# New tokens' share of the samples' values in one product per group, and the conv norm's channel tiles added before the partition sum

## The chip, the cores and the metric

The program runs on one core of a Trainium2 chip. The metric is the device time of one execution in microseconds (us), as the median of several runs. The core has five engines with a queue each: PE multiplies matrices (its weight loads are shown apart, as PEld), DVE and ACT do vector and activation work, POOL does vector work on SBUF only, and SP here issues every DMA. Each engine takes its instructions strictly in the order in which they were written.

## The reference, cut to what matters

One decoder layer is computed for 512 prompt tokens and for 8 samples of 4 new tokens each (32 sample tokens). The sample tokens attend to 2048 cached rows of keys and values and to their own new ones:

```python
h = rms_norm(x, norm_pre); z = h @ w_in          # q | k | v | gate | conv a | conv b | conv gate
# samples: k_all = [cached k, new k], v_all = [cached v, new v]; three dilated patterns,
# their softmaxes merged, so every output is one weighted sum over cached and new values
c = depthwise_causal_conv(u_pad, conv_dw_w, conv_dw_b)      # 512 channels
mu = mean(c); var = mean((c - mu)**2)                       # LayerNorm over the channels
c = silu((c - mu) * rsqrt(var + EPS) * g + b)
mix = concat(att * silu(g_att), (c @ conv_pw_w + conv_pw_b) * silu(g_conv))
y = x + rms_norm(mix @ w_out, norm_post)
```

The output also holds the caches, moved on by four tokens.

## The kernel before, in words

**The main line.** 544 token columns (512 + 32) are projected in 60 column tiles of `w_in` (`project`, L849), each in four steps of 24 matmuls; weights and activations are split into a high and a low part, which makes three matmuls of one. After each step comes a tick (`tick`, L767). In a tick the side generators write a piece of their work into the engines' queues: heads of the prompt's attention (rank 0), the samples' attention (rank 1), the conv branch (rank 2). So PE's queue holds steps of `z` with small pieces between them, and what a piece waits for holds up all that follows. The pieces' dates (`UTK`, `UTV`, the numbers that a generator yields) count ticks, not time.

**The weights.** For each quarter of a weight tile (`split`, L798) ACT casts the high part `wh` (L809) and POOL makes the low part `wl` (L810). Each has four buffers, and ACT and POOL run ahead of PE as far as these allow. In their queues a quarter's two instructions stand where `project` writes them: the third quarter ahead of a tile's first step, the fourth ahead of its second, the next tile's first two ahead of its third and fourth.

**The samples' values** (`v_phase`, L700). There are three groups of four heads. For each group and each of the 8 samples (24 units) PE multiplies the probabilities by the cached values: `kvf` (j = 0 to 2, written in one tick) and `kvm` (j = 3 to 6) and at last the new values `vtm` (j = 7), two ticks later. Each j is four matmuls side by side on 32 columns of the array each; j = 7 has 32 rows only, all samples' new tokens at once, with probabilities that are zero off the sample's own. Four samples fill one PSUM bank `o` (tag `acc`, one buffer). `gather` (L707) then copies the bank to `osb` on ACT (L709), PE turns it (`ot`, L713) and DVE writes the parts to `mixg` (L719).

**The conv norm** (`conv_ln`, L456). `cc` holds four tiles of 128 channels. For each half of the tokens (272 columns), PE sums over the channels by four float32 matmuls with a constant matrix into one bank (`pm`, L469); DVE subtracts the mean (L471); ACT squares (`csq`, L479); four more matmuls sum the squares (`pvar`, L483); ACT copies them (L485). Up to it, DVE makes the depthwise conv tap by tap (L442, L444).

**Bulk copies.** The cached rows are copied DRAM to DRAM in 176 pieces (`bulk`, L321). A tick issues them until the bytes sent reach START + PACE times a count of PE's columns (`mm` adds to it, L105; a float32 matmul counts four times, one with a tile position once).

**The output stage** (L1128 on) multiplies by `w_out`: `oz` for the prompt's tokens, `os` for the samples' (straight from the loaded weights `raw`, L1140).

Of the kernel before, what the change touches and what calls it, by code (L numbers as in the profile page):

```python
# [10 lines left out]
F32 = mybir.dt.float32  # L11
F32R = mybir.dt.float32r
AF = mybir.ActivationFunctionType
ALU = mybir.AluOpType
# [4 lines left out]
P = 128  # L19
# [3 lines left out]
NB = 8  # L23
NT = 4
NS = NB * NT
TOK = SEQ + NS
HT = TOK // 2
NH = 12
G4 = 4
PAST = 2048  # L30
ROW = 2 * NH * P
CW = 31
# [10 lines left out]

UTK, UTV = 3.8, 3.7

START, PACE = 4_000_000, 166.3

NF = 3

# [36 lines left out]
def body(tc, xT, xtok, gpost, w_in, w_out, ckv, cconv, relb, vecs, pww, c_oht, c_ohr, c_lmr, c_tm, c_pick,  # L86
         o_y, o_kvp, o_cp, o_cs, o_kvs):
    nc = tc.nc
# [7 lines left out]
    def dma(out, in_):  # L96
        sent[0] += 4 * math.prod(out.shape)
        return tc.keep_in_program_order(nc.sync.dma_start(out, in_))
# [4 lines left out]
    def mm(out, lhsT, rhs, start, stop, tile_position=None):  # L103
        n = math.prod(rhs.shape[1:])
        pe[0] += n * (1 if rhs.dtype == F32R or tile_position else 4)  # L105
        if tile_position is None:
            nc.tensor.matmul(out, lhsT, rhs, start=start, stop=stop)  # L107
        else:
            nc.tensor.matmul(out, lhsT, rhs, start=start, stop=stop, tile_position=tile_position)  # L109

    def tr(out, in_, eye):
        pe[0] += in_.shape[0] * 2
        nc.tensor.transpose(out, in_, eye)  # L113

    def dma_late(out, in_, delay=5):
        late.append((now[0] + delay, out, in_))
# [51 lines left out]
    def bank(tag, name):  # L168
        return (psz if tag == "z" else psa).tile([P, 512], F32, tag=tag, name=name)
# [15 lines left out]
    def V(o, i=0):  # L185
        return vec[:, o + i:o + i + 1]

    xh, xl = [], []
    ones = keep.tile([P, P], F32, name="ones")
# [46 lines left out]
    apool = ap_.enter_context(tc.tile_pool(name="att", bufs=1))  # L236
# [44 lines left out]
    lt = ip.tile([P, 3, 8, NT], F32, name="lt")  # L281
# [174 lines left out]
    def conv_ln():  # L456
        cc = mixg[3]
        def load_pw(n):
            pw = apool.tile([P, 4, P], F32, tag="pw", name=f"pw{n}")
            dma(pw, pww[:, :, n * P:(n + 1) * P])  # L460
            return pw

        pw = load_pw(1)

        for hf in range(2):
            sl = slice(hf * HT, hf * HT + HT)
            pm = bank("z", f"pm{hf}")
            for ct in range(4):
                mm(pm[:, :HT], ones, cc[:, ct, sl], start=(ct == 0), stop=(ct == 3))  # L469
            for ct in range(4):  # L470
                nc.vector.scalar_tensor_tensor(cc[:, ct, sl], pm[:, :HT], -4.0, cc[:, ct, sl], op0=ALU.mult,  # L471
                                               op1=ALU.add)
            yield
        ri = apool.tile([P, TOK], F32, tag="q", name="cri")
        for hf in range(2):
            sl = slice(hf * HT, hf * HT + HT)
            csq = [apool.tile([P, 2, HT], F32, tag="up", name=f"csq{hf}_{i}", bufs=2) for i in range(2)]
            for ct in range(4):
                nc.scalar.activation(csq[ct // 2][:, ct % 2, :], cc[:, ct, sl], AF.Square)  # L479
            yield  # L480
            pv = bank("z", f"pvar{hf}")
            for ct in range(4):
                mm(pv[:, :HT], ones, csq[ct // 2][:, ct % 2, :], start=(ct == 0), stop=(ct == 3))  # L483
            vs = apool.tile([P, HT], F32, tag="ccv", name=f"vs{hf}")
            nc.scalar.copy(vs, pv[:, :HT])  # L485
            yield
            yield from rsqrt(ri[:, sl], vs, HT, 4.0, apool, tag="up")
            yield
        for ct in range(4):
            nc.vector.tensor_tensor(cc[:, ct, :], cc[:, ct, :], ri, op=ALU.mult)  # L490
            nc.scalar.activation(cc[:, ct, :], cc[:, ct, :], AF.Identity, bias=V(V_LNB, ct), scale=V(V_LNG, ct))
            th = apool.tile([P, TOK], F32, tag="up", name=f"cth{ct}", bufs=2)
            nc.scalar.activation(th, cc[:, ct, :], AF.Tanh, scale=0.5)
            nc.vector.scalar_tensor_tensor(cc[:, ct, :], th, 1.0, cc[:, ct, :], op0=ALU.add, op1=ALU.mult)
            yield

        res = [cc[:, 0, :]] + [apool.tile([P, TOK], F32, tag="up", name=f"pwo{i}", bufs=2) for i in range(2)]
        res.append(apool.tile([P, TOK], F32, tag="q", name="pwo2"))
        for n in (1, 2, 3, 0):
            for hf in range(2):  # L500
                sl = slice(hf * HT, hf * HT + HT)
                ps = bank("z", "pwp")
                for ct in range(4):
                    mm(ps[:, :HT], pw[:, ct, :], cc[:, ct, sl], start=(ct == 0), stop=(ct == 3))
                dst = res[n]
                nc.scalar.activation(dst[:, sl], ps[:, :HT], AF.Identity, bias=V(V_PWB, n), scale=0.5)
                yield
            if n:
                yield
                pw = load_pw((n + 1) % 4)  # L510
                yield
                yield
                yield
        for n in range(1, 4):
            nc.scalar.copy(cc[:, n, :], res[n])
        state["conv"] = True
        yield
# [4 lines left out]
    smp = {}  # L522
# [35 lines left out]
    def tm_take(g, nm, tag):  # L558
        t_ = state["sp"].tile([NS, 512], F32, tag=tag, name=f"{nm}tm{g}", bufs=2 if tag == "qb" else 1)
        nc.scalar.copy(t_, smp[g][nm + "ps"][0:NS, :])  # L560
        off = ((0 if nm == "k" else NH) + g * G4) * P
        dma_late(o_kvs[:, PAST - NT:PAST, off:off + 512], t_)
        smp[g][nm + "tm"] = t_
# [136 lines left out]
    def v_phase(g):  # L700
        sp = state["sp"]
        u0 = g * 16 + 8
        pt = smp[g]["pt"]
        while state.get("v", -1) < 4 * g + 3:
            yield

        def gather(half, o):  # L707
            osb = sp.tile([P, 512], F32, tag="ktn", name=f"osb{g}_{half}")
            nc.scalar.copy(osb, o)  # L709
            yield  # L710
            ps = bank("q", f"ot{g}_{half}")
            for s in range(4):
                tr(ps[:, s * P:s * P + P], osb[:, s * P:s * P + P], ident)  # L713
            yield
            for s in range(4):
                b = half * 4 + s
                src = ps[:, s * P:s * P + P].rearrange("p (h r) -> p h r", h=G4)[:, :, NT * b:NT * b + NT]
                dst = mixg[g][:, :, SEQ + NT * b:SEQ + NT * b + NT]
                nc.vector.tensor_copy(dst, src)  # L719
            yield  # L720

        got = iter(())
        for half in range(2):
            o = bank("acc", f"o{g}_{half}")
            for s in range(4):
                b = half * 4 + s
                u = u0 + b
                load_far(u)
                load_mid(u)
                load_far(u + 1)  # L730
                far, mid = fars[u], mids[u]
                if b < 2:
                    tm_mm(g, "vk"[b])
                for j in range(8):
                    for hh in range(G4):
                        hs = slice(hh * NS, hh * NS + NS)
                        hc = slice(hh * P, hh * P + P)
                        if j < 7:
                            src = far[:, j, hc] if j < 3 else mid[:, j - 3, hc]
                            lt = pt[:, j, hs]  # L740
                        else:
                            src = smp[g]["vtm"][:, hc]
                            lt = pt[0:NS, 7, hs]
                        mm(o[hs, s * P:s * P + P], lt, src, start=(j == 0), stop=(j == 7),
                                         tile_position=(0, hh * NS))
                    if j == 2:
                        yield UTV / 2
                        if b < 2:
                            tm_take(g, "vk"[b], ("vnew", "qb")[b])
                        next(got, None)  # L750
                        load_mid(u + 1)
                if s < 3:
                    yield UTV / 2
                    next(got, None)
            yield UTV / 2 - 1 if half == 0 else 1
            got = gather(half, o)
            next(got)
            yield
        load_far(u0 + 9)
        load_mid(u0 + 9)  # L760
        smp[g]["got"] = got
# [207 lines left out]
    for n in range(N_IN):  # L969
        c = order[n]  # L970
# [6 lines left out]
        if c < 3 * NH:  # L977
            nm = "qkv"[kind]
            g, hh = divmod(h, G4)
# [89 lines left out]
    op = ctx.enter_context(tc.tile_pool(name="outp", bufs=1))  # L1069
# [76 lines left out]
    for c in range(4):  # L1146
        last = c == 3

        for bs in (((0, 1), (2,), (3,)) if last else ((0, 1), (2, 3))):
            tags = ("z", "z") if 0 in bs else ("att", "s") if 2 in bs else ("t",)  # L1150
            z = [bank(t, f"oz{c}_{b}") for b, t in zip(bs, tags)]
            for i in range(KT):
                j = c * KT + i
# [146 lines left out]
```

## Time and profile before

| | |
|---|---|
| median of 3 runs | 1174.95 us (1173.05 to 1175.88) |
| the profiled execution | 1170.97 us, its span 1169.2 us |
| PE busy | 1137.5 us (97%) |
| DVE, POOL, ACT busy | 674.0, 406.8, 378.1 us |
| DMA | 401.92 MB, mean 344 GB/s |
| granted TensorE clock, mean | 0.990 |

Busy time is the union of an engine's instructions. A float32 matmul leaves two records in the trace. In a timeline each row is a run of like instructions: start, length, engine, line, operation, output<-inputs, shape, count, and in brackets how long the engine had been idle and who ended that.

### The profile page before, as it was taken

The page shows a single profiled execution, that of the slowest core. Times are in us where ns is not written, and L with a number is a line of the kernel's source. Part 1 is how long each engine was busy: PE and PEld are TensorE (multiplying, and loading weights), DVE is VectorE, ACT ScalarE, POOL GpSimd, SP SyncE. Part 2 cuts the span into 40 slices and gives each one's busy share as a digit, 9 for nine tenths or more (in the row PEclk, how much of TensorE's full clock was granted, in tenths as well). Part 3 has the DMA queues.
Part 4 walks back from the last instruction along what each step waited for, and adds up shares of the span by engine and source line. Part 5 has one row for each costly group of instructions (what it writes and reads, how often), then busy time and mean ns, then how long its engine had stood idle before and what let it go on. Part 6 is the DMA issues. An engine that isn't in the chain of part 4 may idle for free.

```text
span 1169.2 us, 23598 instructions
## 1 busy us (share of the span) xinstructions
PE 1137.5 (97%) x9322; PEld 1029.4 (88%) x9322; DVE 674.0 (58%) x1997; ACT 378.1 (32%) x749; POOL 406.8 (35%) x353
## 2 busy tenths in 40 slices
PE   7899999999999999999999999999999999999996
PEld 7699999999999999999999999899999976776775
DVE  5209899599699988778233576994222243112136
ACT  5433333422123332331334333423222253223241
POOL 5043323344344333333322222334333445313130
PEclk9989999999999999999999999999999998999999
DMA  9899999999998998999998899889999968999966
GB/s 363 278 339 373 402 351 343 383 312 338 408 329 320 402 381 323 351 362 355 408 375 331 293 384 395 330 317 373 387 386 338 337 218 292 337 357 389 332 232 225
DMA packets 96083, 401.92 MB, mean 344 GB/s; under 512 B 15000, under 2 KB 17816, under 8 KB 89765
## 3 DMA queue, kind: packets, MB, share of 16 engines
q1 hardware_dynamic: 95972, 400.42, 93.6%
q8 instruction: 73, 1.20, 0.4%
q14 instruction: 38, 0.30, 0.1%
HBM read 388.65 MB, written 212.66 MB: 514 GB/s over the span
## 4 chain that ended last, share of the span: by engine, by line
PE 56%; DVE 2%; DMA 1%; issue 1%; POOL 0%; ACT 0%; SPq 0%; DVEq 0%; ACTq 0%; POOLq 0%
PE z L107 32%; PE oz L107 14%; PE o L109 3%; PE pwp L107 1%; PE os L109 1%; PE att L107 1%; DMA raw<-in_w_out_dram 1%; PE s L107 1%; PE t L113 1%; DVE qsc L628 1%; POOL owl L844 0%; PE kt L113 0%; PE pvar L107 0%; PE pm L107 0%; PE sn L109 0%
## 5 line engine op out<-in xcount | busy, mean ns | idle before, releaser
L107 PE MATMUL z<-xh,wh 128*128 128x272 f32 x1920 | 572.3, 298 | 8.7 <-ACT wh L894 7.6
L107 PE MATMUL z<-xh,wl 128*128 128x272 f32 x1920 | 555.0, 289 | 1.1 <-POOL wl L895 0.6
L107 PE MATMUL z<-xl,wh 128*128 128x272 f32 x1920 | 553.4, 288 | 0.0
L810 POOL TENSOR_TENSOR wl<-raw,wh 128x512 fp32r<-128x512 f32 x228 | 311.1, 1374 | 471.3 <-ACT wh L809 447.7
L107 PEld LDWEIGHTS z<-xh,wh 128*128 128x128 f32 x1920 | 363.6, 189 | 25.2 <-issue 11.0
L107 PEld LDWEIGHTS z<-xl,wh 128*128 128x128 f32 x1920 | 363.2, 189 | 1.6 <-issue 1.0
L107 PEld LDWEIGHTS z<-xh,wl 128*128 128x128 f32 x1920 | 363.0, 189 | 1.8 <-POOL wl L895 0.9
L809 ACT CAST wh<-raw 128x512 fp32r<-128x512 f32 x228 | 139.1, 617 | 181.4 <-PE z L107 106.4
L334 DVE TENSOR_TENSOR t<-z,R 128x272 f32<-128x272 f32 x96 | 42.0, 439 | 181.5 <-PE z L107 170.2
L628 DVE SCALAR_TENSOR_TENSOR qsc<-kvf,qb 128x128 f32<-128x128 f32 x288 | 125.6, 436 | 8.8
L628 DVE SCALAR_TENSOR_TENSOR qsc<-kvm,qb 128x128 f32<-128x128 f32 x288 | 112.4, 390 | 8.8
L442 DVE SCALAR_TENSOR_TENSOR mix<-up,vec,mix 128x512 f32<-128x512 f32 x120 | 107.6, 896 | 0.0
L107 PE MATMUL oz<-owl,mh 128*128 128x512 f32 x256 | 101.7, 397 | 3.7 <-POOL owl L844 3.7
L107 PE MATMUL oz<-owh,mh 128*128 128x512 f32 x256 | 103.4, 404 | 1.5 <-ACT owh L843 1.5
L107 PE MATMUL oz<-owh,ml 128*128 128x512 f32 x256 | 101.3, 396 | 0.0
L844 POOL TENSOR_TENSOR owl<-raw,owh 128x512 fp32r<-128x512 f32 x43 | 61.4, 1447 | 111.2 <-ACT owh L843 81.8
L107 PEld LDWEIGHTS oz<-owh,mh 128*128 128x128 f32 x256 | 48.5, 189 | 26.4 <-issue 8.4
L844 DVE TENSOR_TENSOR owl<-raw,owh 128x512 fp32r<-128x512 f32 x21 | 21.7, 1032 | 73.0 <-ACT owh L843 72.8
L107 PEld LDWEIGHTS oz<-owl,mh 128*128 128x128 f32 x256 | 48.7, 190 | 15.6 <-POOL owl L844 4.1
L843 ACT CAST owh<-raw 128x512 fp32r<-128x512 f32 x64 | 36.8, 618 | 78.3 <-DMA raw<-in_w_out_dram 69.4
L107 PEld LDWEIGHTS oz<-owh,ml 128*128 128x128 f32 x256 | 48.4, 189 | 10.6
L444 DVE SCALAR_TENSOR_TENSOR mix<-us,vec,mix 128x32 f32<-128x32 f32 x120 | 57.0, 475 | 0.0
(180 smaller groups left out, 991.7 us busy)
## 6 DMA issues: line engine op xcount, KB each, us to landing
out_dram<-in_ckv_dram SPq DMA_DIRECT2D x168, 1152.0 KB, 12.2
raw<-in_w_in_dram SPq DMA_DIRECT2D x119, 512.0 KB, 9.7
kvm<-in_ckv_dram SPq DMA_DIRECT2D x48, 1024.0 KB, 10.5
kvf<-in_ckv_dram SPq DMA_DIRECT2D x144, 256.0 KB, 8.2
raw<-in_w_out_dram SPq DMA_DIRECT2D x32, 512.0 KB, 9.1
out_dram<-t SPq DMA_DIRECT2D x24, 256.0 KB, 9.2
mix<-in_xtok_dram SPq DMA_DIRECT2D x4, 1024.0 KB, 14.0
xt<-in_xtok_dram SPq DMA_DIRECT2D x8, 512.0 KB, 4.7
```

Of the source, the lines that this page charges most:

```text
L107: nc.tensor.matmul(out, lhsT, rhs, start=start, stop=stop)
L109: nc.tensor.matmul(out, lhsT, rhs, start=start, stop=stop, tile_position=tile_position)
L113: nc.tensor.transpose(out, in_, eye)
L334: nc.vector.tensor_tensor(dst[:, sl], z[hf][:, :HT], R[:, sl], op=ALU.mult)
L442: nc.vector.scalar_tensor_tensor(cc[:, ct, :SEQ], up[:, j:j + SEQ], wj, cc[:, ct, :SEQ], op0=ALU.mult, op1=ALU.add)
L444: nc.vector.scalar_tensor_tensor(cs, us[:, :, j:j + NT], wj, cs, op0=ALU.mult, op1=ALU.add)
L628: nc.vector.scalar_tensor_tensor(scr, src[:, hh * P:hh * P + P], SCALE, qb[:, hh * P:hh * P + P], op0=ALU.mult, op1=ALU.mult, accum_out=sd ...
L809: nc.scalar.copy(wh, raw)
L810: nc.gpsimd.tensor_tensor(wl, raw, wh.bitcast(F32), op=ALU.subtract)
L843: nc.scalar.copy(wh, raw)
L844: (nc.vector if j % 3 == 2 else nc.gpsimd).tensor_tensor(wl, raw, wh.bitcast(F32), op=ALU.subtract)
```

## The change

Three things change. In `v_phase` the part j = 7 is taken out of all 24 units; it is computed once for each group, for all samples, in unit b = 3 ahead of j = 0 (`new_mm`, into a bank of tag `q`), copied by ACT to a new tile `ov`, and added in `gather`: where ACT copied the bank `o`, DVE now adds `ov` to each of its four parts. In `conv_ln` POOL adds the four channel tiles (three adds, `total`, in two buffers of tag `us`), and PE sums over the partitions with one matmul in place of four. PACE goes from 166.3 to 167.9.

```diff
@@ -43,7 +43,7 @@
 
 UTK, UTV = 3.8, 3.7
 
-START, PACE = 4_000_000, 166.3
+START, PACE = 4_000_000, 167.9
 
 NF = 3
 
@@ -460,13 +460,21 @@
             dma(pw, pww[:, :, n * P:(n + 1) * P])
             return pw
 
+        def total(parts, name):
+
+            a = apool.tile([P, NB * (NT + CW - 1)], F32, tag="us", name=f"ca{name}", bufs=2)[:, :HT]
+            b = apool.tile([P, NB * (NT + CW - 1)], F32, tag="us", name=f"cb{name}", bufs=2)[:, :HT]
+            nc.gpsimd.tensor_tensor(a, parts[0], parts[1], op=ALU.add)
+            nc.gpsimd.tensor_tensor(b, parts[2], parts[3], op=ALU.add)
+            nc.gpsimd.tensor_tensor(a, a, b, op=ALU.add)
+            return a
+
         pw = load_pw(1)
 
         for hf in range(2):
             sl = slice(hf * HT, hf * HT + HT)
             pm = bank("z", f"pm{hf}")
-            for ct in range(4):
-                mm(pm[:, :HT], ones, cc[:, ct, sl], start=(ct == 0), stop=(ct == 3))
+            mm(pm[:, :HT], ones, total([cc[:, ct, sl] for ct in range(4)], f"m{hf}"), start=True, stop=True)
             for ct in range(4):
                 nc.vector.scalar_tensor_tensor(cc[:, ct, sl], pm[:, :HT], -4.0, cc[:, ct, sl], op0=ALU.mult,
                                                op1=ALU.add)
@@ -479,8 +487,8 @@
                 nc.scalar.activation(csq[ct // 2][:, ct % 2, :], cc[:, ct, sl], AF.Square)
             yield
             pv = bank("z", f"pvar{hf}")
-            for ct in range(4):
-                mm(pv[:, :HT], ones, csq[ct // 2][:, ct % 2, :], start=(ct == 0), stop=(ct == 3))
+            mm(pv[:, :HT], ones, total([csq[ct // 2][:, ct % 2, :] for ct in range(4)], f"v{hf}"), start=True,
+               stop=True)
             vs = apool.tile([P, HT], F32, tag="ccv", name=f"vs{hf}")
             nc.scalar.copy(vs, pv[:, :HT])
             yield
@@ -706,7 +714,8 @@
 
         def gather(half, o):
             osb = sp.tile([P, 512], F32, tag="ktn", name=f"osb{g}_{half}")
-            nc.scalar.copy(osb, o)
+            nc.vector.tensor_tensor(osb.rearrange("p (s c) -> p s c", s=4), o.rearrange("p (s c) -> p s c", s=4),
+                                    ov[:, None, :].to_broadcast([P, 4, P]), op=ALU.add)
             yield
             ps = bank("q", f"ot{g}_{half}")
             for s in range(4):
@@ -720,6 +729,17 @@
             yield
 
         got = iter(())
+
+        ov = sp.tile([P, P], F32, tag="ov", name=f"ov{g}")
+
+        def new_mm():
+            ps = bank("q", f"ov{g}")
+            for hh in range(G4):
+                hs = slice(hh * NS, hh * NS + NS)
+                mm(ps[hs, 0:P], pt[0:NS, 7, hs], smp[g]["vtm"][:, hh * P:hh * P + P], start=True, stop=True,
+                   tile_position=(0, hh * NS))
+            return ps
+
         for half in range(2):
             o = bank("acc", f"o{g}_{half}")
             for s in range(4):
@@ -731,22 +751,21 @@
                 far, mid = fars[u], mids[u]
                 if b < 2:
                     tm_mm(g, "vk"[b])
-                for j in range(8):
+                if b == 3:
+                    new = new_mm()
+                for j in range(7):
                     for hh in range(G4):
                         hs = slice(hh * NS, hh * NS + NS)
                         hc = slice(hh * P, hh * P + P)
-                        if j < 7:
-                            src = far[:, j, hc] if j < 3 else mid[:, j - 3, hc]
-                            lt = pt[:, j, hs]
-                        else:
-                            src = smp[g]["vtm"][:, hc]
-                            lt = pt[0:NS, 7, hs]
-                        mm(o[hs, s * P:s * P + P], lt, src, start=(j == 0), stop=(j == 7),
+                        src = far[:, j, hc] if j < 3 else mid[:, j - 3, hc]
+                        mm(o[hs, s * P:s * P + P], pt[:, j, hs], src, start=(j == 0), stop=(j == 6),
                                          tile_position=(0, hh * NS))
                     if j == 2:
                         yield UTV / 2
                         if b < 2:
                             tm_take(g, "vk"[b], ("vnew", "qb")[b])
+                        if b == 3:
+                            nc.scalar.copy(ov, new[:, 0:P])
                         next(got, None)
                         load_mid(u + 1)
                 if s < 3:
```

## Rows read from the trace of the kernel before

**Rows 1.** The page's first lines: span, and busy time of each engine.

```profile
span 1169.2 us, 23598 instructions
PE 1137.5 (97%) x9322; PEld 1029.4 (88%) x9322; DVE 674.0 (58%) x1997; ACT 378.1 (32%) x749; POOL 406.8 (35%) x353
```

**Rows 2.** Waits of PE: for whom, us in total, times, longest.

```profile
PE z L107 <- ACT wh L894: 7.6, 1, 7.6
...
PE os L109 <- DMA raw<-in_w_out_dram: 0.2, 1, 0.2
```

**Rows 3.** Timeline of PE, stretches around units of the samples' values.

```profile
239.32 0.86 PE L109 MATMUL o<-kvf,spt 128*32 128x128 f32 x24
240.11 0.39 PE L107 MATMUL z<-xh,wh 128*128 128x272 f32 x1
...
246.29 1.08 PE L109 MATMUL o<-kvm,spt 128*32 128x128 f32 x32
247.30 0.42 PE L109 MATMUL o<-vtm,spt 32*32 32x128 f32 x8
247.65 0.39 PE L107 MATMUL z<-xh,wh 128*128 128x272 f32 x1
...
295.00 0.86 PE L109 MATMUL o<-kvf,spt 128*32 128x128 f32 x24
```

**Rows 4.** Groups of PE by shape: count, busy us, mean ns, idle before.

```profile
L107 PE MATMUL pm<-mix,ones 128*128 128x272 f32 x16 | 4.1, 399 | 0.0
```

**Rows 5.** Timeline of PE, the conv norm's sums.

```profile
555.79 2.10 PE L107 MATMUL pm<-mix,ones 128*128 128x272 f32 x8
...
560.75 1.99 PE L107 MATMUL pm<-mix,ones 128*128 128x272 f32 x8
...
570.12 2.00 PE L107 MATMUL pvar<-csq,ones 128*128 128x272 f32 x8
...
590.85 2.10 PE L107 MATMUL pvar<-csq,ones 128*128 128x272 f32 x8
```

**Rows 6.** Timeline of POOL around the conv norm.

```profile
548.20 1.47 POOL L810 TENSOR_TENSOR wl<-raw,wh 128x512 fp32r<-128x512 f32 x1 [0.22 <-ACT wh L809]
554.23 1.28 POOL L810 TENSOR_TENSOR wl<-raw,wh 128x512 fp32r<-128x512 f32 x1 [4.56 <-ACT wh L809]
...
564.89 1.28 POOL L810 TENSOR_TENSOR wl<-raw,wh 128x512 fp32r<-128x512 f32 x1 [7.89 <-ACT wh L809]
...
590.67 0.21 POOL L1027 COPY sk<-t 128x32 f32<-128x32 f32 x1 [6.32 <-DVE t L334]
```

**Rows 7.** Timeline of DVE: a half's end, and the conv taps' end.

```profile
289.07 0.43 DVE L997 TENSOR_TENSOR mix<-z,R 128x272 f32<-128x272 f32 x1
...
548.45 1.27 DVE L444 SCALAR_TENSOR_TENSOR mix<-us,vec,mix 128x32 f32<-128x32 f32 x1
...
550.31 0.24 DVE L444 SCALAR_TENSOR_TENSOR mix<-us,vec,mix 128x32 f32<-128x32 f32 x1
```

**Rows 8.** Timeline of ACT, the second half's squares.

```profile
581.10 1.39 ACT L479 ACTIVATE csq<-mix 128x272 f32<-128x272 f32 x4
```

**Rows 9.** Groups of POOL, DVE and ACT by shape.

```profile
L1020 POOL COPY smix<-mix 128x128 f32<-128x128 f32 x3 | 0.8, 306 | 0.0
...
L677 DVE TENSOR_TENSOR srow<-pa,srow 128x512 f32<-128x512 f32 x3 | 2.0, 680 | 0.0
...
L376 ACT COPY pt<-t 128x128 f32<-128x128 f32 x12 | 3.2, 264 | 7.3 <-PE t L113 7.1
```

**Rows 10.** Stretch of the output stage: busy us by engine, clock, DMA share, GB/s.

```profile
1000.00:1100.00 100.00, 99.79 (x450) 73.04 (x449) 21.37 (x27) 28.85 (x58) 28.23 (x21) 1.00 0.99 359
```

**Rows 11.** Chain of waits in the output stage: start, us, what.

```profile
1059.27 11.57 DMA raw<-in_w_out_dram
...
1070.88 1.05 PE os L109 x4
```

**Rows 12.** The page's DMA issues: count, KB each, us to landing.

```profile
out_dram<-in_ckv_dram SPq DMA_DIRECT2D x168, 1152.0 KB, 12.2
```

## The prediction

> **What bounds the kernel now.** I read the page's first lines, then PE's waits, then PE's timeline at the two places that change, then POOL's, DVE's and ACT's timelines there, and last the transfers.
>
> PE is busy for 1137.5 of 1169.2 us [rows 1], so all its idle time is 31.7 us. The longest single wait is 7.6 us, at the start, for the first cast weights; in the whole execution PE itself lost 0.2 us to a transfer [rows 2]. The reader is to see that no other engine holds PE up between the ramp and the last rows: POOL and ACT are busy for a third, DVE for 58% [rows 1]. Time taken off PE's queue should therefore come off the end, as long as nothing that PE waits for comes later than now.
>
> **1. The new tokens' part leaves the units.** In the timeline of one unit the four cached parts j = 3 to 6 take 246.29 to 247.30, and j = 7 takes 247.30 to 247.65, when the next weight matmul starts: 0.35 us [rows 3]. Do the four parts get dearer when z follows them directly? Three parts that are followed by z take 239.32 to 240.11, 0.79 us or 0.264 each with the turn to z in it; four at that price are 1.05, against 1.01 now [rows 3]. So a unit saves 0.31 to 0.35 us; I take 0.35, since the 1.01 us hold a turn already (to j = 7). The code makes 24 units of three groups and eight samples: 8.4 us gone, 7.4 at the low price.
>
> Added are three times the same eight records, between a z and a j = 0 part, which has no like in the trace. From below: eight records at the mean price of the 32, a quarter of 1.01 us, 0.25; from above: the 0.35 us of j = 7, and once more the 0.1 us by which it exceeds that quarter, 0.45. I take 0.35, the row of the same records: 1.05 us. Net 6.0 to 7.7 us, I take 7.4.
>
> The Trainium skill, TensorEngine Tiling (Array Packing), Tiling Modes, says that a change of the tiling mode drains the engine, and this speaks against a block of its own shape between two others. The trace agrees in so far as the 0.35 us of j = 7 exceed that quarter [rows 3]; by the rule each block costs the 0.45, and the net is 7.1 us.
>
> The copy of `ov` is a 128x128 copy from PSUM on ACT, 0.26 us [rows 9], three times, in an engine that is busy for 32%; its reader comes two ticks later at least. In `gather` ACT's copy becomes an add on DVE, 128x512 with an input in PSUM: 0.68 us by the nearest row [rows 9], six times, 4.1 us. What hides it: DVE must have read the bank before the next unit's first matmul. At the first half's end the next part starts at 295.00, and the last values, written two ticks ahead (7.0 us from 239.32 to 246.29) and 1.36 us long, are done by about 289.4 [rows 3], and DVE is then just past its 289.07 item, ahead of a tick's taps [rows 7]; in DVE's order the add falls right behind that item, so it ends at about 290.2, 4.8 us early. Behind the add wait three pairs of taps and the second half's scaling; PE needs that bank a tile later. Cost taken: nothing; without that cover at most 6 x 0.7 = 4 us.
>
> **2. The conv norm.** Each sum is eight records. The second one shows their step: 1.99 us [rows 5], of which the last record takes 0.40 [rows 4], so seven steps in 1.59, 0.228 us each. Six go: 1.37 us; four sums [rows 5] make 5.5 us. The first sum, 2.10 us, gives steps of 0.24 and 5.8 us; all eight records spread over 1.7 us give 0.21 and 5.1.
>
> Added are twelve POOL adds of 128x272 float32. The trace has none on POOL. Bounds: below, a 128x128 copy, 0.31 us [rows 9]; above, a 128x512 subtraction, 1.28 us, or 1.47 us while DVE runs taps [rows 6]. The second is the same kind of instruction with 1.9 times the columns: 0.68 us, I take 0.7, so 2.1 us for a sum's three. PE now waits for POOL, and all of PE's queue stands behind that wait; POOL in turn must have the inputs, must be past the weight part written ahead of the tick, and for the second sum on must wait until PE has read the buffer two adds back. Place by place, before PE gets there:
>
> - First mean: POOL is free at 549.67 (548.20 + 1.47) and next busy at 554.23 with a weight part that stands behind the tick [rows 6]; the last tap ends at 550.55 [rows 7]. Adds end near 552.0, PE arrives at 555.79 [rows 5]: 3.8 us early.
> - Second mean: the part of 554.23 ends at 555.51; the buffer is free when PE has done the first sum, about 556.4; adds end at 558.5. PE arrives 1.37 earlier than now, 559.4: 0.9 early at 0.7 us, 0.8 late at 1.28 us.
> - First variance: behind the part of 564.89 [rows 6], moved up by two sums to 562.15 to 563.4; adds end at 565.5; PE arrives at 570.12 - 2.74 - 0.35 = 567.0: 1.5 early.
> - Second variance: squares end at 582.5 [rows 8], and POOL is idle from 584.35 to 590.67 [rows 6]. All of this moves up by some 4.5 us with PE, the adds end about 4 us early.
>
> So at 0.7 us nothing is late; at 1.28 us some 1 us is lost. The weight parts behind the adds slip by up to 4 us and are used by PE only two steps, 6 us, later. I take 5.5 less 0.1: 5.4 us.
>
> **3. PACE.** The count falls by 84 x 128 columns for the samples and 12 x 272 x 4 for the norm, 23,808, of some 2.3 million (an estimate: the z, oz and os records alone are 2 million): 1.0%, and PACE rises by 0.96%. So the copies end at the same place of the program, in 1% less time. This matters where transfers are close: in the output stage the DMA share is 0.99 at 359 GB/s [rows 10], and the chain of waits runs through one weight load of 11.57 us that lands just as PE needs it [rows 11]; PE lost 0.2 us there [rows 2]. A copy is 1152 KB [rows 12], 3.3 us at that rate. If one falls ahead of such a load where now it falls behind, PE waits about 3 us. Bounds: nothing, or once in each of four column groups, 12 us. Only one load has no slack in the chain, and copies come neither more nor fewer, so I take less than half of one copy: 1.3 us lost.
>
> **Sum.** 7.4 + 5.4 - 1.3 = 11.5 us. The profiled execution took 1170.97 us (1.8 around its span) and would take 1159.5. It lies 4.0 us below the median of the runs, 1174.95; I carry that over: 1163.4 us.
>
> **Rivals.**
> - *Weight loads late in the output stage.* For it: the rows of part 3. Against it: one bare load, 0.2 us of waiting. If all four column groups lose 3 us, 12.8 - 12 leaves 1174, no change. Chance 0.08; one or two such stalls are in my own range.
> - *The transfers are the bound*, and PE's gain becomes waiting. For it: a DMA share of 0.99. Against it: 0.2 us of PE's waits in the whole execution [rows 2]. Then about 1174.5. Chance 0.04.
> - *POOL's adds hold up PE: slower.* Place: the four sums. If the adds begin only when PE is there (behind a weight part of 1.28 us, or held by DVE's taps) and cost 1.47 each, PE waits 1.28 + 3 x 1.47 = 5.7 us at each. That less the 1.37 gained, four times, is 17.3 us lost; with 7.4 gained it gives 1185. It decides from 3.2 us of waiting per sum on (7.4/4 + 1.37); my times have the adds 0.9 to 4 us early. Against it: POOL's gaps [rows 6]. For it: a weight part goes from 1.28 to 1.47 beside taps, and a small tap beside one from 0.24 to 1.27 us [rows 6, 7]. Chance 0.04. The Trainium skill, SBUF — State Buffer, Who interferes with whom, makes this a rule: a DVE instruction with two SBUF inputs and a POOL instruction that reads SBUF block one another for the whole instruction. The trace's 1.27 us agrees; by that rule only the first mean's adds meet taps, and it has the most room.
>
> **How the numbers follow.** The forecast has 0.84, the rivals 0.08, 0.04 and 0.04. The range takes the bounds: 7.7 + 5.8 with nothing lost gives 1161.4, and 1.4 for the runs' own spread (half of 1173.05 to 1175.88) gives 1160; 6.0 + 4.4 with a stall and a half, 4.9 us, gives 1169.5. A change below 0.3%, 3.5 us, can't be told from none here. Faster 0.87 (the forecast, and the milder half of the first rival), same 0.08, slower 0.05.
>
> **What would show it.** PE busy less by 12 to 13 us; o<-vtm records down from 192 to 24 under a new name, each block about 0.35 us; pm and pvar with four records each and no idle PE ahead of them; adds on POOL of 0.7 us that end before PE arrives; DVE's add of 0.68 us before the next unit's matmul. Wrong would be: a wait of PE for POOL's adds of over 1 us, os waiting for raw by several us, or units that stay at 1.36 us.

## The result, and the profile after

| | before | after |
|---|---|---|
| median of the runs compared | 1174.81 us (1173.05 to 1175.88) | 1167.03 us (1166.48 to 1169.81) |
| ratio, with its 95% interval | | 0.9944 [0.9927, 0.9961] |
| profiled execution, its span | 1170.97, 1169.2 us | 1169.68, 1167.9 us |

Faster, by 7.8 us between the medians; 11.5 us were forecast. The profiled execution of the changed kernel is among the slowest of its runs (so is that of c0, its repeat below), so the spans alone show only 1.3 us of it.

The head of the changed kernel's page, and its waits of PE (for whom: us in total, times, longest):

```profile
span 1167.9 us, 23238 instructions
...
PE 1128.8 (97%) x9130; PEld 1024.6 (88%) x9130; DVE 681.5 (58%) x2003; ACT 375.5 (32%) x746; POOL 417.0 (36%) x365
```

```profile
PE z L107 <- ACT wh L913: 8.9, 1, 8.9
...
PE os L109 <- DMA raw<-in_w_out_dram: 5.1, 2, 3.7
...
PE z L107 <- POOL wl L829: 1.0, 2, 0.5
```

PE's busy time fell by 8.7 us instead of 12 to 13, and two waits grew: `os` waits 5.1 us for its weights where it waited 0.2 [rows 2], and `z` waits for POOL's weight parts twice where it did once. No wait for POOL's new adds is among them.

**The two edits themselves.** PE's timeline of the changed kernel, at a group's new block, at a unit's end, and at the four sums of the norm:

```profile
282.17 0.42 PE L109 MATMUL ov<-vtm,spt 32*32 32x128 f32 x8
282.52 0.86 PE L109 MATMUL o<-kvf,spt 128*32 128x128 f32 x24
...
289.53 1.08 PE L109 MATMUL o<-kvm,spt 128*32 128x128 f32 x32
290.54 0.39 PE L107 MATMUL z<-xh,wh 128*128 128x272 f32 x1
...
556.50 0.73 PE L107 MATMUL pm<-cam,ones 128*128 128x272 f32 x2
...
560.06 0.62 PE L107 MATMUL pm<-cam,ones 128*128 128x272 f32 x2
...
567.72 0.62 PE L107 MATMUL pvar<-cav,ones 128*128 128x272 f32 x2
...
586.69 0.73 PE L107 MATMUL pvar<-cav,ones 128*128 128x272 f32 x2
```

A unit's second block now takes 1.01 us to the next `z` (290.54 - 289.53) where it took 1.36 [rows 3]; the new block takes 0.35. The sums have two records where they had eight [rows 5]. POOL's last add of each sum (timeline of POOL) ends before PE gets there:

```profile
553.93 0.79 POOL L469 TENSOR_TENSOR cam<-cam,cbm 128x272 f32<-128x272 f32 x1
...
558.16 0.78 POOL L469 TENSOR_TENSOR cam<-cam,cbm 128x272 f32<-128x272 f32 x1
...
565.65 0.77 POOL L469 TENSOR_TENSOR cav<-cav,cbv 128x272 f32<-128x272 f32 x1
...
582.07 0.77 POOL L469 TENSOR_TENSOR cav<-cav,cbv 128x272 f32<-128x272 f32 x1
```

The margins are 1.8, 1.1, 1.3 and 3.9 us (556.50 - 554.72, and so on). Of the two other added operations, DVE's add in `gather` takes 0.68 us, six times, and ACT's copy of `ov` 0.26 us, three times.

**Where the time went, stage by stage.** PE's `z` records count 96 to a column tile, so the first record of a tile marks its start. Lengths in us of the stages so cut, for the two kernels, for a repeat of the changed one (c0) and for five of the variants below:

| stage | before | after | c0 | a1 | a3 | a4 | c1 | c2 |
|---|---|---|---|---|---|---|---|---|
| start, to tile 4 | 74.45 | 77.25 | 78.36 | 76.74 | 78.00 | 76.00 | 78.73 | 74.70 |
| tiles 14 to 21 (group 0's values) | 119.79 | 117.35 | 117.35 | 117.35 | 117.35 | 119.79 | 118.01 | 118.01 |
| tiles 22 to 31 (group 1's keys) | 157.76 | 158.80 | 158.80 | 158.80 | 158.81 | 157.76 | 158.22 | 158.21 |
| tiles 32 to 39 (group 1's values, norm) | 135.25 | 127.20 | 127.20 | 127.20 | 132.74 | 129.70 | 127.20 | 127.20 |
| tile 50 to the first `oz` (group 2's values) | 142.05 | 139.65 | 139.65 | 139.65 | 139.65 | 142.05 | 139.65 | 139.65 |
| output, first to last `oz` | 205.62 | 213.43 | 211.64 | 205.93 | 206.14 | 206.12 | 204.76 | 204.91 |

The stages shown between start and output repeat to a few hundredths of a us from profile to profile, where the same code runs in them. There the change takes off 2.44 + 8.05 + 2.40 us and adds 1.04: 11.85 us, close to the 12.8 forecast without PACE. The start varies by chance (74.4 to 78.7 us over all profiles of the study, and nothing of the change lies in it). In the output stage 7.8 us come back.

**What comes back in the output stage.** The chain of waits of the changed kernel (start, us, what), around the longer of the two `os` waits:

```profile
966.72 17.43 DMA out_dram<-in_ckv_dram
...
984.22 24.84 DMA raw<-in_w_out_dram
...
1009.11 1.05 PE os L109 x4
```

The load of the 12th half tile of `w_out` is issued at 984.22 and lands 24.84 us later. PE stood there from 1005.4 (1009.11 less the wait of 3.7). For the kernel before, the same load and its landing, in the view of the tile `raw` at 988 to 990 us:

```profile
L98 SPq DMA_DIRECT2D raw<-in_w_out_dram x1: 333/333/333, 989.2 to 989.2; - x1
...
DMA to landing us min/median/max: 22.9/22.9/22.9
```

It landed at 1012.1, and the chain of that kernel has its use in the second half of this piece, from 1013.9 on:

```profile
1013.52 0.99 PE os L109 x8
```

So a load that was 1.8 us early (24.7 us from issue to use, 22.9 needed) became 3.7 late (21.2 and 24.84). SP's timeline says what stands ahead of it (start, length, what, count), before and after:

```profile
972.37 0.52 SPq L98 DMA_DIRECT2D out_dram<-in_ckv_dram  x1
...
973.61 7.18 SPq L98 DMA_DIRECT2D out_dram<-in_ckv_dram  x7
...
985.33 0.51 SPq L98 DMA_DIRECT2D out_dram<-in_ckv_dram  x1
```

```profile
963.42 1.15 SPq L98 DMA_DIRECT2D out_dram<-in_ckv_dram  x2
...
965.24 7.27 SPq L98 DMA_DIRECT2D out_dram<-in_ckv_dram  x6
...
976.73 4.74 SPq L98 DMA_DIRECT2D out_dram<-in_ckv_dram  x2
```

Ten copies where there were nine. That count doesn't set the length of the wait by itself: c0, b4 and a3 below have ten at this place too, and PE waits 1.0, 0.6 and 0.3 us there. By the chain SP then stood until 984.14, when a copy issued at 966.72 had landed; why it waits for that, no run tells. The 28th half tile, the place of the second wait, also has one copy more ahead of it in SP's order.

PE then runs slower for a while after the wait. The output stage has four column groups, and most `os` records stand in the first half of each. In the view of stretches the length stands first, then PE's busy time; PEclk, DMA share and GB/s stand last. First the changed kernel, then the one with PACE back (a1), each for that half of the second and of the fourth group:

```profile
1002.90:1035.00 32.10, 28.43 (x122) 19.60 (x121) 6.84 (x9) 9.56 (x20) 9.74 (x7) 0.95 0.93 337
...
1108.16:1136.56 28.40, 26.92 (x121) 18.43 (x120) 7.99 (x9) 9.55 (x20) 9.78 (x7) 1.00 0.71 257
```

```profile
1002.60:1028.50 25.90, 25.90 (x122) 18.30 (x121) 6.84 (x9) 9.47 (x20) 9.81 (x7) 1.00 0.97 361
...
1101.36:1128.44 27.08, 26.94 (x121) 18.43 (x120) 7.00 (x9) 9.34 (x20) 9.74 (x7) 1.00 0.98 357
```

The same work takes 32.10 us instead of 25.90. By PE's rows 3.7 of the 6.2 us are the wait, and 2.5 are PE's own records (28.43 against 25.90). About 1.0 of these 2.5 is there at the full clock too, with shorter waits: in both fourth stretches PE is busy for 26.9 us, at a granted clock of 1.00. PE's rows show too little of a wait, since their ends are modelled; the row of the weight loads has 4.58 us for this one:

```profile
1009.11 0.14 PEld L109 LDWEIGHTS os<-raw,smix 128*32 128x32 f32 x4 [4.58 <-DMA raw<-in_w_out_dram]
```

The other 1.5 us go with the mean granted clock of 0.95. The view of stretches, cut finer, shows the clock after the wait's end:

```profile
1009.11:1010.60 1.49, 1.49 (x6) 0.60 (x7) 0.29 (x1) 1.36 (x3) 0.76 (x1) 1.00 0.71 297
1010.60:1014.00 3.40, 3.40 (x9) 2.69 (x9) 1.07 (x1) 0.92 (x2) 3.40 (x3) 0.51 1.19 463
```

PE had been idle for 3.7 us, worked for 1.5 at the full level (2.4 GHz), and was then granted the half (1.2 GHz) for 3.4 us. The transfers are no busier where PE waits: their share is 0.93 and 0.71 in the two stretches of the changed kernel, 0.97 and 0.98 in those of a1.

### The profile page after: what moved, and what is told of

It reads as the page before. It is cut to its first block, busy times and chain, and to the rows that moved or that the text cites. A ratio compares the mean times of both kernels' runs of the same rounds, so it can differ in the third digit from the quotient of the medians.

```text
span 1167.9 us, 23238 instructions
## 1 busy us (share of the span) xinstructions
PE 1128.8 (97%) x9130; PEld 1024.6 (88%) x9130; DVE 681.5 (58%) x2003; ACT 375.5 (32%) x746; POOL 417.0 (36%) x365
## 4 chain that ended last, share of the span: by engine, by line
PE 51%; DMA 6%; DVE 1%; issue 1%; ACT 1%; POOL 1%; SPq 0%; DVEq 0%; POOLq 0%; ACTq 0%
PE z L107 32%; PE oz L107 10%; DMA raw<-in_w_out_dram 5%; PE o L109 2%; DMA out_dram<-in_ckv_dram 1%; PE pwp L107 1%; PE att L107 1%; PE s L107 1%; PE os L109 1%; PE t L113 1%; POOL owl L863 1%; DVE qsc L636 1%; SPq L98 0%; PE kt L113 0%; PE sn L109 0%
## 5 line engine op out<-in xcount | busy, mean ns | idle before, releaser
L444 DVE SCALAR_TENSOR_TENSOR mix<-us,vec,mix 128x32 f32<-128x32 f32 x120 | 62.9, 524 | 0.0
```

Source lines behind the costliest of these rows:

```text
L444: nc.vector.scalar_tensor_tensor(cs, us[:, :, j:j + NT], wj, cs, op0=ALU.mult, op1=ALU.add)
```

## The experiments

**a1: PACE back.** The first four kernels part the three edits.

```diff
-START, PACE = 4_000_000, 167.9
+START, PACE = 4_000_000, 166.3
```

> The changed kernel with PACE back at 166.3. Theory A (one bulk copy more ahead of a late weight load): in the order of SP's issues nine copies then stand ahead of the 12th and of the 28th half tile of w_out (between the 6th and the 12th load, and between the 25th and the 28th), as in the kernel before, where the changed kernel has ten each time. PE's waits of os for raw go from 5.1 us to under 1 us and the clock stays up there: about 1161 to 1163 us. Theory B (the transfers as a whole bind, so PE's gain is worth about 60%): 1166 to 1168 as the changed kernel, os waits or others staying at some 5 us. Three copies more are left for the end (4 for 1): if they are not hidden there, up to 10 us more.

Measured: 1161.59 us (1161.32 to 1163.01) beside 1173.81 before, ratio 0.990 [0.9884, 0.9915]. Nine copies stand ahead of both half tiles again, `os` waits at neither, and the output stage is 205.93 us. Without its PACE the change is worth 12.2 us.

**a2: the kernel before with the new PACE.**

```diff
-START, PACE = 4_000_000, 166.3
+START, PACE = 4_000_000, 167.9
```

> The kernel before with PACE 167.9 alone. Theory A: nine copies ahead of the 12th and 28th half tile, as before, so no new wait: 1174 to 1176, the same as before. Theory B, the transfers bind and PACE pushes 1% more of them into each stretch: slower by some 3 to 5 us, 1178 to 1180.

Measured: 1173.28 us, ratio 1.0002 [0.9993, 1.0011]. The same number costs nothing where the columns counted are those of the kernel before. What hurts is a place in SP's order, not a higher rate.

**a3: the samples' part alone, PACE 167.9** (the norm as before: `conv_ln` without `total`).

```diff
...
-            mm(pm[:, :HT], ones, total([cc[:, ct, sl] for ct in range(4)], f"m{hf}"), start=True, stop=True)
+            for ct in range(4):
+                mm(pm[:, :HT], ones, cc[:, ct, sl], start=(ct == 0), stop=(ct == 3))
...
```

> Only the samples' part (conv norm as before, PACE 167.9). The z stages gain 7.4 us in both theories. Theory A: ten copies ahead of the 12th half tile, nine ahead of the 28th, so one wait of os for raw of 3 to 4 us with a clock loss of 1 to 2 us: 1171 to 1173. Theory B: 60% of 7.4, so 1170.5, with the loss spread.

Measured: 1168.11 us, 0.9953 [0.9941, 0.9966]. The three stages with values gain 2.44, 2.51 and 2.40 us, and the stage of tiles 22 to 31 is 1.05 longer: that loss belongs to the samples' part. The wait of 3 to 4 us that I expected didn't come, and the time is below both theories. Ten copies do stand ahead of the 12th half tile, as SP's timeline shows; but PE's wait there is 0.3 us:

```profile
969.45 0.52 SPq L98 DMA_DIRECT2D out_dram<-in_ckv_dram  x1
...
970.68 6.66 SPq L98 DMA_DIRECT2D out_dram<-in_ckv_dram  x7
...
982.21 3.75 SPq L98 DMA_DIRECT2D out_dram<-in_ckv_dram  x2
```

```profile
PE os L109 <- DMA raw<-in_w_out_dram: 0.3, 1, 0.3
```

The load is issued 23.2 us before PE wants it and takes 23.5, where these were 21.2 and 24.84 in the changed kernel. What makes the difference between the two, no run tells.

**a4: the norm's part alone, PACE 167.9** (the units with j = 7 again, ACT's copy in `gather`; the lines are against the changed kernel).

```diff
...
-                for j in range(7):
+                for j in range(8):
...
```

> Only the conv norm's adds on POOL (samples' part as before, PACE 167.9). Theory A: nine copies ahead of both half tiles, so the whole 5.5 us arrive: 1169 to 1170, os waits under 1 us, no PE wait for POOL's adds. Theory B: 60% of it, 1171.5. If POOL's adds held PE up, pm and pvar would show idle PE ahead of them and the gain would be under 3 us.

Measured: 1168.33 us, 0.9949 [0.9936, 0.9961]. The norm's stage is 5.55 us shorter, the other stages between start and output are as before. Nine copies stand ahead of both half tiles, and `os` waits 0.5 us at another one (the 22nd); the time is a little under the 1169 to 1170 of theory A.

**b1: the add on POOL instead of DVE**, PACE 166.3. It tests whether DVE's adds make the 1.04 us.

```diff
-            nc.vector.tensor_tensor(osb.rearrange("p (s c) -> p s c", s=4), o.rearrange("p (s c) -> p s c", s=4),
+            nc.scalar.copy(osb, o)
+            nc.gpsimd.tensor_tensor(osb.rearrange("p (s c) -> p s c", s=4), osb.rearrange("p (s c) -> p s c", s=4),
                                     ov[:, None, :].to_broadcast([P, 4, P]), op=ALU.add)
```

> The changed kernel with PACE 166.3, and in gather the bank copied by ACT as before the change, with POOL adding ov in SBUF. Theory C: in the first group's units DVE is full of conv taps, so each 0.68 us add on it makes DVE's queue later; ACT waits behind it for the last q columns, the weights' casts behind that, and PE loses 0.73 us at the start of the second group and 0.30 us some 30 us on. With the adds off DVE both go: 1160.6, about 1.0 us under the 1161.6 of the kernel with PACE 166.3. Rival D: the loss comes from PE being earlier (2 us) against the same DVE work, and the add has no part: no change, 1161.6. Rival E: POOL's 1.3 us adds wait for ACT ahead of weight parts and PE waits for these instead: 1162 or more.

Measured: 1163.81 us, 0.991 [0.9893, 0.9926]. The stage of tiles 22 to 31 grew to 159.37 us, where theory C has it come back with DVE free of the adds. The norm's stage grew too, to 128.64 us from the 127.20 of a1: one of the new adds stands in POOL's queue ahead of a sum's adds, and PE waits for that sum, close to what rival E had. POOL's timeline, then PE's:

```profile
566.66 1.28 POOL L718 TENSOR_TENSOR osb<-osb,ov 128x512 f32<-128x512 f32 x1 [1.30 <-ACT osb L717]
```

```profile
570.28 0.72 PE L107 MATMUL pvar<-cav,ones 128*128 128x272 f32 x2 [1.17 <-POOL cav L469]
```

Two of the six adds stood among DVE's taps, 1.4 us; without them the taps took 2.0 us more than in the changed kernel (170.4 against 168.4 in all), so DVE had no less to do. The Trainium skill, SBUF — State Buffer, Who interferes with whom, has a DVE instruction with two SBUF inputs contend with a POOL instruction that reads SBUF. The 2.0 us would fit; but the taps take 164.6 us before and 166.3 in c1, both without a POOL add of this kind, so no run here shows that the adds made them. b1 left the question of the 1.04 us open; c1 takes it up.

**b3: one copy held** until the 12th half tile of `w_out` is issued, and one until the 28th is; PACE 167.9 as in the change.

```diff
+HOLD = ((11, 148), (27, 172))
...
+            if any(d2d_at[0] >= cap and 2 * NTILE + m not in raws for m, cap in HOLD):
+                return
```

> The changed kernel, PACE 167.9 as it is, but one bulk copy held back until the 12th half tile of w_out has been issued, and one until the 28th: 9 and 9 copies ahead instead of 10 and 10, all else the same. Theory A (the tenth copy makes the load late): os waits for raw go from 5.1 us to under 1 us, 1162 to 1163. If the loss of the changed kernel is spread or comes from PACE by another way (theory B): no change, 1166 to 1168.

Measured: 1162.29 us (1159.45 to 1163.25), 0.9899 [0.988, 0.9917]; no wait of `os`, the output stage 206.70. Two copies moved by a few places give the time of a1, at the PACE of the change.

**b4: one copy drawn ahead** of the 12th half tile, in the kernel of a1.

```diff
+        if m == 2 * NTILE + 11:
+            bulk(sent[0] + 1)
```

> The kernel with PACE 166.3 (1161.6 us), with one copy drawn ahead of the 12th half tile of w_out, 10 instead of 9 there, and one fewer just behind it. Theory A: PE waits 1 to 4 us for that load, as with the ten copies of the two kernels that had them (0.9 and 3.7 us), 1163 to 1166, and the rest of the trace is the same. Theory B: no change, 1161.6.

Measured: 1162.37 us (1159.8 to 1165.48), 0.9909 [0.989, 0.9927]. PE's wait:

```profile
PE os L109 <- DMA raw<-in_w_out_dram: 0.6, 1, 0.6
```

The wait comes back at that half tile and the stretch is 1.6 us longer than in a1 (27.49 against 25.89), less than I expected. As in a3, the tenth copy alone uses up the slack there and costs a short wait.

**b5: three further adds on POOL in each sum**, in the kernel of a1 (the sums are then other values). It measures the room that POOL's adds have.

```diff
+            for _ in range(3):
+                nc.gpsimd.tensor_tensor(a, a, b, op=ALU.add)
```

> The kernel with PACE 166.3, with three further adds on POOL in each of the conv norm's four sums (it adds parts of the channels more than once, so the norm is another). Theory F: POOL's three adds of 0.77 us end only 1 to 2 us before PE needs the first three sums, so 2.3 us more per sum costs PE about 0.5, 3 and 0 to 1 us, and nothing at the fourth (4 us of room): 1165 to 1166. Rival: POOL's chain has room for it in each place, 1161.6.

Measured: 1167.80 us, 0.9949 [0.9929, 0.9969], above the 1165 to 1166 expected. PE's timeline at the first three sums, with the idle time before them and who ended it:

```profile
554.43 0.73 PE L107 MATMUL pm<-cam,ones 128*128 128x272 f32 x2 [0.71 <-POOL cam L471]
...
560.50 0.73 PE L107 MATMUL pm<-cam,ones 128*128 128x272 f32 x2 [2.35 <-POOL cam L471]
...
569.55 0.73 PE L107 MATMUL pvar<-cav,ones 128*128 128x272 f32 x2 [1.14 <-POOL cav L471]
```

2.4 us more on POOL per sum cost 4.2 us of waiting at three of the four, and the stage is 4.8 us longer (132.0 against 127.2). The room at those three is 1 to 2 us, as the margins in the changed kernel's profile have it.

**c0: the changed kernel once more**, beside c1 and c2 on one chip.

> The changed kernel once more, unaltered. Theory A (the place of the copies in SP's queue makes the output stage's waits): the column groups of the output stage repeat as in its first profile, near 32 and 28 us for the second and the fourth (25.9 where no copy is early), os waits for raw by 4 to 6 us in two waits, time 1166 to 1170. Rival: that profile caught a chance of its own; then the stage is near 206 us, os waits for under 1 us, and the time is near 1162, as with PACE back.

Measured: 1166.21 us (1164.89 to 1169.22), 0.9937 [0.992, 0.9953]. The wait of `os`, and the second and fourth stretches:

```profile
PE os L109 <- DMA raw<-in_w_out_dram: 3.1, 2, 2.2
```

```profile
1004.41:1032.32 27.91, 26.93 (x121) 18.43 (x120) 6.84 (x9) 9.55 (x20) 9.41 (x7) 1.00 1.03 383
...
1105.33:1135.82 30.49, 28.34 (x122) 19.57 (x121) 7.96 (x9) 9.56 (x20) 9.74 (x7) 0.94 0.64 240
```

The two waits stand at the same half tiles again, with the same ten copies ahead of each, and the stage is 211.64 us. Which of them is the longer changed (1.0 and 2.2 us here), and the lower clock went with the longer one; the waits' total, 3.1, is below the 4 to 6 that I expected of a pattern that repeats.

**c1: in group 0 no add on DVE's path**, PACE 166.3. The new values are made turned there, and join in the small copies that DVE makes anyway.

```diff
+            if g:
+                nc.vector.tensor_tensor(osb.rearrange("p (s c) -> p s c", s=4), o.rearrange("p (s c) -> p s c", s=4),
+                                        ov[:, None, :].to_broadcast([P, 4, P]), op=ALU.add)
+            else:
+                nc.scalar.copy(osb, o)
...
+                    new = ov.rearrange("p (h r) -> p h r", h=G4)[:, :, NT * b:NT * b + NT]
+                    nc.vector.tensor_tensor(dst, src, new, op=ALU.add)
...
+                if g == 0:
+                    mm(ps[:, hs], smp[g]["vtm"][:, hh * P:hh * P + P], pt[0:NS, 7, hs], start=True, stop=True)
+                    continue
```

> The change with PACE 166.3; in group 0 alone ACT copies the bank as before, the new values' part is made turned (channel by row) and is added by DVE within the small copies to the mixer tile, so that DVE has no 0.68 us adds there. Theory C (those two adds make DVE late in group 0, DVE's squares for the key norm late, and with them casts and POOL's weight parts): the stage of column tiles 22 to 31 falls from 158.8 back to about 157.8, and the time lies some 1.0 us less up to 0.6 (dearer weight loads of the turned product) under the change with PACE back: 1160.6 to 1161.5. Rival D (PE is simply early there, by 2.4 us, and DVE full of taps): the stage stays at 158.8, 1161.6 or more.

Measured: 1160.88 us (1158.66 to 1163.16), 0.9888 [0.9871, 0.9905]. The stage of tiles 22 to 31 is 158.22: 0.58 of the 1.04 us went. But the turned product costs 0.66 us in the stage before (118.01), so PE comes to tile 22 later by that much and gains nothing in sum. DVE's `sq`, on which PE's new idle time hangs (see the step on the add below), comes no earlier without the adds:

```profile
358.09 0.17 DVE L1029 TENSOR_TENSOR sq<-z,R 128x32 f32<-128x32 f32 x1
```

Counted from the start of tile 14 (235.41 here, 233.93 in the changed kernel, 231.13 before) it comes at 122.7 us, as in the changed kernel (122.6); before it was 123.5. So c1 doesn't show that the adds make the loss. It fits rival D, by which PE is early against DVE's work: with PE 0.66 us later the loss is smaller by about as much. Its column counts don't move the copies: they stand as in a1.

**c2: c1 with three copies issued early**, in the gap of the transfers at the start of the output stage.

```diff
+    bulk(sent[0] + 3 * 1_170_000)
```

> As the kernel with the turned part in group 0, and three bulk copies are issued early, at the start of the output stage ahead of the load of the conv norm's vectors, where the transfers have a gap, so that fewer stand ahead of the late w_out half tiles. Theory A: the last waits in the output stage go, it falls from 205.9 to about 205 us, the time to about 1160. Rival: the first w_out half tiles come late behind the three copies, PE waits there by 1 us or more, and the stage is 207 or more, time 1162 or more.

Measured: 1160.17 us (1157.76 to 1162.23), 0.9883 [0.9865, 0.9901]; output stage 204.91. The weight loads of `os` stand for 0.65 and 0.80 us at the first half tiles, too little for the rival's 207 us, so it falls; but c1 has no wait of `os` left either (204.76), and the two can't be told apart. The test was empty: the 1.2 us that I meant to take from a1's last stretch (27.08 us against 25.90) are gone in c1 already, and why, no run tells. They were a wait for weights, which PE's rows nearly hide (0.14 us) and the row of the weight loads shows, in a1:

```profile
1110.82 0.14 PEld L109 LDWEIGHTS os<-raw,smix 128*32 128x32 f32 x4 [1.05 <-DMA raw<-in_w_out_dram]
```

The variants of the whole change with nine copies or fewer ahead of both half tiles and no further work on POOL (a1, b3, c1, c2) are all faster than the changed kernel. For c1 and c2 that is shown on one chip beside c0: the ranges don't meet, and by the medians they win 5.3 and 6.0 us.

## Why the prediction was right in sign and 3.7 us too large

**Step 1, the units: right in size.** 7.4 us forecast, 2.44 + 2.51 + 2.40 = 7.35 measured (a3). The block of its own costs 0.35 us three times, the value taken. The Trainium skill, TensorEngine Tiling (Array Packing), Tiling Modes, has a change of mode drain the engine; by it I had put the block at 0.45. The trace shows 0.35, so nothing beyond what the row of j = 7 held already.

**Step 1, "Cost taken: nothing" for what waits in DVE's queue: wrong by 1.04 us.** The cover that I named held: the add ends before the next unit needs the bank. But I wrote that "three pairs of taps and the second half's scaling" wait behind the add and priced only the scaling's bank, not the rest of DVE's queue. In tiles 14 to 21 DVE is busy for 109.9 of 117.4 us (before: 107.0 of 119.8). DVE's timeline of the changed kernel, then ACT's and PE's:

```profile
349.31 0.68 DVE L717 TENSOR_TENSOR osb<-o,ov 128x512 f32<-128x512 f32 x1
...
356.55 0.18 DVE L1019 TENSOR_TENSOR sq<-z,R 128x32 f32<-128x32 f32 x1
```

```profile
356.76 0.62 ACT L595 COPY qsc<-sq 128x512 f32<-128x512 f32 x1 [6.30 <-DVE sq L1019]
357.29 1.66 ACT L828 CAST wh<-raw 128x512 fp32r<-128x512 f32 x3
```

```profile
359.74 0.40 PE L107 MATMUL z<-xh,wl 128*128 128x272 f32 x1 [0.47 <-POOL wl L829]
```

And the same of the kernel before, DVE and ACT:

```profile
354.60 0.18 DVE L1000 TENSOR_TENSOR sq<-z,R 128x32 f32<-128x32 f32 x1
```

```profile
354.81 0.62 ACT L587 COPY qsc<-sq 128x512 f32<-128x512 f32 x1 [4.71 <-DVE sq L1000]
355.34 1.14 ACT L809 CAST wh<-raw 128x512 fp32r<-128x512 f32 x2
```

Tile 22 starts on PE at 350.92 before and at 351.28 after. DVE's `sq` comes 3.7 us after that before, 5.3 after. ACT waits for it, its casts stand behind the copy, POOL's parts behind the casts, and PE idles 0.47 us where it didn't idle at all. That link is seen in the trace, and with it tile 22 takes 0.73 us more; another 0.30 us go at the turns of `v` in tile 24 (0.85 instead of 0.53 us). What makes `sq` late against PE stays open. From the start of tile 14 on PE gains 2.44 us and `sq` only 0.85, and in c1, without the adds, `sq` gains no more; the 0.30 us are there in c1 too. It would fit that PE reaches DVE's work 2.4 us earlier; no run parts that from the adds. Either way the premise that "no other engine holds PE up between the ramp and the last rows" held for the kernel before, and not for one whose PE comes earlier.

**Step 2, the norm: right in size and in its covers.** 5.4 forecast, 5.55 measured (a4; 5.54 between a3 and a1). POOL's adds took 0.77 us where 0.7 was taken. PE found each sum made by 1.8, 1.1, 1.3 and 3.9 us, where 3.8, 0.9, 1.5 and 4 were forecast. The first was off because its second add waited for the last tap. The rival in which these adds hold up PE did not come; b5 shows it with 2.4 us more per sum.

**Step 3, PACE, "less than half of one copy: 1.3 us lost": right mechanism, size wrong, and the term that made the error.** It cost 7.5 us in the profile (213.43 - 205.93), 5.7 in c0's, and 4.4 to 4.6 by the medians, each beside the kernel before of its own comparison (12.2 us of a1 less 7.8, and less 7.7 of c0). I had looked for loads without slack in the chain of before, found one, and taken the odds of a copy falling ahead of it. Three things were missing. The chain shows only loads with no slack: the 12th half tile's had 1.8 us, which is less than one copy's 3.3. The place of each copy could have been worked out, since the count decides it before the run: it puts one more ahead of the 12th and the 28th half tile, in the changed kernel and in c0 alike. And a wait there costs more than PE's rows show of it (6.2 us for one of 3.7), since these hide about 1.0 us and PE's clock fell behind it. Holding back just these two copies (b3) gives the time of a1, so their place is shown to be the cause; why ten copies make a wait of 3.7 us in one kernel and of 0.3 in another (a3) is not. By that step, the output stage's first rival (1174 us, four stalls) had the right place, with two stalls instead of four. The range holds the result because its far end had a stall and a half, 4.9 us, in it; the 1.3 us of the forecast were odds, not a reading.

The sum with what was measured: 7.35 - 1.04 + 5.55 less 4.4 to 4.6 is 7.3 to 7.5 us; the medians have 7.8 in the first comparison and 7.7 in c0's.

**Signs named.** PE's busy time fell by 8.7 us, not 12 to 13; in a1 it is 1125.3, 12.2 less, and 2.5 of the difference are the longer records around the 3.7 us wait. `vtm` records, POOL's adds and DVE's add are as forecast. "os waiting for raw by several us" was named as the sign of error, and came.

## What to carry to other kernels

When an edit changes a counter that other things are scheduled by, work out the new order before anything else: here the loads that PE will want soon, against the number of bulk copies issued ahead of each. The count tells which load is at risk, not how late it will be. A load with 2 us of slack doesn't show in the chain of waits; look up its landing against its use. And when PE is to come earlier to an engine that is nearly full in that stretch, or an instruction is added to that engine, follow its whole queue to the next reader on another engine, not only to the reader of the edit's own buffer.

## What the runs showed that I had not expected

- A wait of PE of 3.7 us cost 6.2 us, one of 2.2 us 4.6 (30.49 - 25.90), one of 1.5 us 2.5 (28.40 - 25.90), one of 1.0 us 2.0 (27.91 - 25.90). In the first two the mean granted clock of the stretch was 0.95 and 0.94, in the last two 1.00: there the 1.0 us above the wait is what PE's rows hide of it.
- A 512 KB load took 22.9 us from issue to landing behind nine copies of 1152 KB (before), and 23.5 (a3) and 24.84 behind ten; the median of such loads on the profile's page is 9.1 before and 9.7 after.
- The order of 168 copies, moved by 1% of a count, is worth 0.4% of the program's time with the change and nothing without it (a2: 1.0002).
